# Probabilities, values and sums of squares as pairs of float32r halves in a three-block transformer kernel

## The chip, the core and the metric

The kernel runs on one core of a Trainium2 chip. The core has a matrix engine (TensorE, in the profile PE, with its weight loads as PEld), a vector engine (VectorE, DVE), a scalar engine (ScalarE, ACT), a general engine (GpSimd, POOL) and a queue that starts transfers (SyncE, SP). Each engine runs its own instructions in the order in which they were written; a semaphore makes one wait for another. Products are made in eight banks of PSUM, all else lies in SBUF. The metric is the device time of one execution in microseconds, as the median of several runs.

## The reference, cut to what matters

512 tokens of 1024 features pass through two layers of a first block and one layer of a second. The parts that the change touches are these:

```python
def rmsnorm(x, g, eps=EPS):
    y = xf * lax.rsqrt(jnp.mean(xf * xf, axis=-1, keepdims=True) + eps)
    return y * g
def memory_attention(q, mem_n, w_mem_kv, q_gain, k_gain):      # both layers, 4 heads of 64, 256 memory tokens
    kv = einsum('bmd,de->bme', mem_n, w_mem_kv)
    qh, k = rmsnorm(q, q_gain), rmsnorm(k, k_gain)
    p = softmax(einsum('bshd,bmhd->bhsm', qh, k) * 64 ** -0.5)
    o = einsum('bhsm,bmhd->bshd', p, v)
def diff_attention(q1, q2, k1, k2, v, lam):                    # second layer, 6 heads, values of 128 features
    p = softmax(mask(s1)) - lam * softmax(mask(s2))            # per tile of 128 queries, keys up to the diagonal
    o = einsum('bhqk,bkhe->bqhe', p, v)
# then o = rmsnorm(o, subln) per head; x = x + [o, memory o] @ w_o; x = x + squared-relu mlp(rmsnorm(x))
```

The second block (a convolution, a stick-breaking attention and a gated mlp) is computed by the same kernel; the change does not touch its arithmetic.

## The kernel before

Values lie feature-major, [128 features, 512 tokens]. Nearly every product of a weight matrix is made from float32r halves: a value x is held as a high half (x rounded to float32r, written by ScalarE in `high`) and a low half (x minus the high half, written by VectorE in `low`), and `mm3` adds three products, high by high, high by low and low by high. The weights come from memory in chunks of 128 x 1024 (tile `wr`), and `cut` makes their halves (`wh`) the same way, with three such tiles in flight. A chunk with the products on it is a unit; units run in a fixed order.

Some products are left in plain float32, one instruction in the program and two in the trace each. Among these are, in the first block: the sums of squares of the residual's norm (`norm_end`, tile `ms`, 512 columns, five times), of the keys' norm (`k_norm`, tile `hms` from the selecting constant `sel`, two per pair of key tiles), of the heads' output norm at the end of `diff_item` (tile `dms`), and probabilities by values in `mem_item` (tile `mpv`, values `mv`) and `diff_item` (tile `dpv`, values `v`). Probabilities come out of a transpose on PE (tile `ptr`) and are copied by ACT into `pT` for two tiles of tokens.

Stage B, the mixer of the second layer, is the place that the prediction is about. Its units are, in this order (`B_ORDER`): keys and queries of two pairs of heads (tile `k`, two times 48 + 48 products of 512 columns), the values of four heads (tile `v`, 96 + 96 products of 256 columns), the memory queries (48), keys and queries of the third pair (48 + 48), the last values (96), and then two parts of the output projection w_o (tile `g`): the part of heads 0 to 3 and of the memory attention (144 products), and the part of heads 4 and 5 (48). The first part of w_o needs the outputs of heads 0 to 3 and of the memory attention: its unit calls `need` on their flags before its first product is written into the program.

The order of the work beside the units is made by a planner when the program is built. Attention is written as generators (`diff_item`: one head, one tile of 128 queries, 24 of them; `mem_item`: two heads, one tile of tokens, 8 of them; `k_norm`, `q_norm`, `rope` and others), each of which yields a condition with `when`: tiles that it needs, and how many PSUM banks (`b=`) or tiles of SBUF (`u=`) must be free. After each slice of a unit's products `step` lets those go on whose condition holds at the planner's own estimate of time. Items wait in a queue, at most five are in flight (`INB`), and a new one needs nine free tiles (`ROOM`) of the 67 (`NSLOT`). Where a unit calls `need`, `until` writes the remaining steps of the generators one after another until the flags are set, with no product of a unit between them.

Of the kernel before, what the change touches and what calls it, by code (L numbers as in the profile page):

```python
# [9 lines left out]
F32 = mybir.dt.float32  # L10
F32R = mybir.dt.float32r
# [18 lines left out]
# columns of the packed per-partition vectors  # L30
# [12 lines left out]
# constants that follow from the shapes: for all phases, and for the two attention mixers  # L43
# [43 lines left out]
# the rotation's partners within 32 rows, where a pair of heads has its rotated features: 48 to 64 of one, 64 to 80 of the other  # L87
# [5 lines left out]
# the order of the chunks in the two attention mixers  # L93
# [21 lines left out]
class Token:  # L115
    """Counts a tile of a pool as in use for as long as something holds it."""
# [9 lines left out]
class View:  # L126
    """A tile or a part of one."""
# [22 lines left out]
class Engine:  # L150
    """An engine that also estimates when its instructions end (ns): the order of the work follows from that."""
# [4 lines left out]
    def cost(self, name, out, ins):  # L156
# [5 lines left out]
        # operands with one value per partition besides the tensors  # L162
# [32 lines left out]
class Chunk:  # L195
    """A half of a chunk of weights in tiles of 512 columns."""
# [9 lines left out]
class Unit:  # L206
    """A chunk of weights and the tensor engine's work on it, in slices."""
# [5 lines left out]
class K:  # L213
    def __init__(self, ctx, tc, a, out, stage=99):
# [12 lines left out]
        # emission: units, generators beside them with what each waits for, and queued ones  # L227
# [26 lines left out]
    def pair(self, n=T, s="s"):  # L254
        """A value's high and low halves in float32r."""
# [24 lines left out]
    def drop(self, *banks):  # L280
        """After the last instruction that uses these banks."""
# [35 lines left out]
    def spawn(self, g):  # L317
        """Work that goes on beside the chunks: a generator, a part of it whenever what it waits for is there."""
# [48 lines left out]
    def until(self, test, soft=False):  # L367
        """Goes on with the work beside the chunks until test() holds; soft: or nothing can go on."""
# [20 lines left out]
    def written(self, *tiles):  # L389
        """The tiles' values are under way: instructions that read them may follow."""  # L390
# [57 lines left out]
    def split_later(self, to, src, scale=None, f=None):  # L448
        """The halves, each when what it is made from is there."""
# [16 lines left out]
    def came(self, t, n):  # L466
        """A tile with n words per partition that a load brings."""
# [3 lines left out]
    def cut(self, c):  # L471
        """A chunk of weights as high and low halves; a gain goes by blocks of columns."""
# [30 lines left out]
    def mm3(self, ps, w, x, first, last, **kw):  # L503
        """ps += w.T @ x, each given as (high, low)."""
# [36 lines left out]
    def gemm_k(self, aps, n, xs, m, evac, gain=None, need=(), room=0):  # L541
        """Units that go over the contraction, [128 features, 512] in m banks."""
# [23 lines left out]
    def gemm_v(self, aps, xs, V, keys, gain=None, need=()):  # L566
        """Units for 256 features of the values with tokens on partitions, in two banks; V[key of 128 features, tile]."""
        st = {"d": 0}
        for c, ap in enumerate(aps):
            def body(w, c=c):  # L570
# [15 lines left out]
                if c == len(aps) - 1:  # L586
                    self.need(*need)
                    vs = [self.tmp(s="v") for j in range(2)]
                    for j in range(4):
                        v = vs[j // 2][:, j % 2 * M:(j % 2 + 1) * M]  # L590
                        self.act.activation(v, ps[j], AF.Copy, scale=self.tr[:, j:j + 1])
                        for n, key in enumerate(keys):
                            V[key, j] = v[:, n * P:(n + 1) * P]
# [1407 lines left out]
```

## Time and profile before

| | |
|---|---|
| time, median of 3 runs (lowest, highest) | 1780.07 us (1778.24, 1781.4) |
| span of the profiled execution | 1778.9 us |
| PE busy | 1756.0 us, 99% of the span, 8550 instructions |
| PEld busy | 1453.2 us, 82% |
| DVE busy | 1035.9 us, 58%, 1729 instructions |
| ACT busy | 764.4 us, 43% |
| HBM | 97 GB/s over the span |

The span runs from the first to the last instruction of the profiled execution; the median of the runs lies 1.2 us above it. Busy time is what an engine spent on instructions, with overlaps counted once; the ends of products are modelled, so that the distance from one start to the next tells more than a product's own duration. All arithmetic instructions are written through one helper and carry its line, L177, so the tiles' names tell them apart. "TILE<-A,B" is the tile that is written and what it is read from.

### The profile page before, as it was taken

Reading aid. Unit: us, or ns where it says so; the run is one execution under the profiler, and the core shown is the slowest. Engines: PE = TensorE matmul, PEld = TensorE weight load, DVE = VectorE, ACT = ScalarE, POOL = GpSimd, SP = SyncE. Lnnn points to the kernel's source line nnn. Section 1 sums busy time; section 2 is a strip of 40 time slices with the busy share of each in tenths; the row PEclk is TensorE's granted clock in tenths of the full one; section 3 lists DMA queues with packets and bytes.
Section 4 is the critical chain, followed back from the end, with each engine's and each line's share of the span. In section 5 each row is a group of like instructions: output and inputs, shape, how many; then the busy total and the mean of one; then the engine's idle time right before and its main releaser. Section 6 shows DMA issues by size and latency. Waiting matters only on the chain.

```text
span 1778.9 us, 21781 instructions
## 1 busy us (share of the span) xinstructions
PE 1756.0 (99%) x8550; PEld 1453.2 (82%) x8550; DVE 1035.9 (58%) x1729; ACT 764.4 (43%) x1371; POOL 0.2 (0%) x4
## 2 busy tenths in 40 slices
PE   8999999999999999999999999999999999999997
PEld 7888888888887887887888888887878988888887
DVE  7765654444455777857453535578984753244446
ACT  7543422222234678654222223457676632232234
POOL 0000000000000000000000000000000000000000
PEclk9999999999999999999999999999989999999998
DMA  5423222233233311152323222431112332232232
GB/s 202 141 70 96 95 95 95 97 99 101 95 116 127 104 48 45 57 195 96 95 95 100 101 96 95 142 98 48 60 48 83 99 127 96 95 103 97 95 108 94
DMA packets 57415, 175.71 MB, mean 99 GB/s; under 512 B 6752, under 2 KB 10080, under 8 KB 57312
## 3 DMA queue, kind: packets, MB, share of 16 engines
q1 hardware_dynamic: 57312, 174.32, 29.7%
q8 instruction: 67, 1.10, 0.2%
q14 instruction: 36, 0.29, 0.1%
HBM read 162.50 MB, written 10.22 MB: 97 GB/s over the span
## 4 chain that ended last, share of the span: by engine, by line
PE 96%; ACT 2%; DVE 1%; DMA 0%; SPq 0%; issue 0%; DVEq 0%; ACTq 0%
PE g L177 74%; PE k L177 8%; PE v L177 3%; PE z L177 2%; PE dsc L177 2%; PE mkv L177 1%; PE spv L177 1%; PE ptr L177 1%; PE mpv L177 1%; PE hms L177 1%; PE dpv L177 1%; PE ms L177 1%; ACT ez L177 0%; PE msc L177 0%; PE dms L177 0%; DMA x<-xd 0%
## 5 line engine op out<-in xcount | busy, mean ns | idle before, releaser
L177 PE MATMUL g<-xnh,wh 128*128 128x512 f32 x2176 | 687.9, 393 | 0.0
L177 ACT ACTIVATE wh<-wr 128x1024 fp32r<-128x1024 f32 (+2 forms) x259 | 271.5, 1048 | 650.5 <-PE g L177 490.2
L177 PEld LDWEIGHTS g<-xnh,wh 128*128 128x128 f32 x2176 | 410.4, 189 | 86.0 <-issue 0.7
L177 PE MATMUL g<-xnl,wh 128*128 128x512 f32 x1088 | 425.2, 391 | 1.7 <-DVE xnl L177 1.7
L177 PE MATMUL g<-ush,wh 128*128 128x512 f32 (+1 forms) x1304 | 400.3, 387 | 0.0
L177 DVE TENSOR_TENSOR wh<-wr,wh 128x1024 fp32r<-128x1024 f32 (+2 forms) x259 | 312.9, 1208 | 122.2 <-ACT wh L177 122.2
L177 PEld LDWEIGHTS g<-ush,wh 128*128 128x128 f32 x1304 | 244.2, 188 | 49.8
L177 PE MATMUL g<-usl,wh 128*128 128x512 f32 (+1 forms) x652 | 252.4, 387 | 0.0
L177 PEld LDWEIGHTS g<-xnl,wh 128*128 128x128 f32 x1088 | 205.4, 189 | 45.3 <-DVE xnl L177 2.5
L177 DVE TENSOR_TENSOR x<-x,g 128x512 f32<-128x512 f32 x88 | 60.2, 686 | 204.1 <-PE g L177 204.1
L177 DVE SCALAR_TENSOR_TENSOR u<-g,nr 128x512 f32<-128x512 f32 x84 | 58.0, 691 | 170.0 <-PE g L177 169.8
L177 PEld LDWEIGHTS g<-usl,wh 128*128 128x128 f32 x652 | 122.4, 188 | 25.0
L177 PE MATMUL k<-xnh,wh 128*128 128x512 f32 (+1 forms) x352 | 113.1, 390 | 5.7 <-ACT wh L177 5.7
L177 PEld LDWEIGHTS k<-xnh,wh 128*128 128x128 f32 x352 | 65.8, 192 | 20.5 <-ACT wh L177 5.7
L177 DVE SCALAR_TENSOR_TENSOR y<-glu,vec,y 128x510 f32<-128x510 f32 (+28 forms) x116 | 79.4, 728 | 0.9 <-ACT y L177 0.9
L177 ACT ACTIVATE ush<-u 128x512 fp32r<-128x512 f32 (+1 forms) x88 | 54.6, 623 | 36.3 <-DVE u L177 36.3
L177 PE MATMUL g<-Eh,wh 128*128 128x512 f32 (+1 forms) x208 | 67.2, 387 | 0.0
L177 PE MATMUL k<-xnl,wh 128*128 128x512 f32 (+1 forms) x176 | 66.3, 377 | 0.0
L177 PE MATMUL v<-wh,xnh 128*128 128x256 f32 x320 | 61.3, 291 | 0.0
L177 DVE TENSOR_TENSOR usl<-u,ush 128x512 fp32r<-128x512 f32 (+1 forms) x88 | 58.7, 671 | 0.0
L177 PEld LDWEIGHTS v<-wh,xnh 128*128 128x128 f32 x320 | 49.7, 191 | 1.3 <-issue 0.8
L177 ACT ACTIVATE g<-g 128x512 f32<-128x512 f32 (+1 forms) x24 | 14.3, 596 | 78.6 <-DVE g L177 78.6
(282 smaller groups left out, 2036.0 us busy)
## 6 DMA issues: line engine op xcount, KB each, us to landing
wr<-in_w_up SPq DMA_DIRECT2D x84, 512.0 KB, 3.4
wr<-in_w_down SPq DMA_DIRECT2D x80, 512.0 KB, 3.4
wr<-in_w_gate SPq DMA_DIRECT2D x20, 512.0 KB, 3.4
wr<-in_a_w_in SPq DMA_DIRECT2D x16, 512.0 KB, 3.9
wr<-in_w_in SPq DMA_DIRECT2D x16, 512.0 KB, 3.5
xd<-x SPq DMA_DIRECT2D x31, 256.0 KB, 2.0
x<-xd SPq DMA_DIRECT2D x31, 256.0 KB, 4.8
wr<-in_w_o SPq DMA_DIRECT2D x10, 512.0 KB, 3.5
```

The source lines that it names most:

```text
L177: r = f(out, *args, **kw)
```

## The change

Probabilities and values in both attentions of the first block become pairs of float32r halves, and their products become `mm3`, three float32r products for one float32 product. The values' low halves (`vl`, `mvl`) and the probabilities' low halves (the second half of `pT`) are new VectorE instructions that read PSUM. The sums of squares of full width (`ms`, `hms` of the keys, `dms`) are first split by a new generator `halves` (tile `hl`, one ACT and one DVE instruction of 512 columns and a `when` between them) and are then made by `mm2`, two float32r products against a constant in float32r. In `k_norm` the two key tiles are split one after the other. A pair of 512 columns takes two of the 67 tiles where a float32 value took one, so the values of stage B take twelve tiles in place of six, each layer's memory values two in place of one. `pT` grows from 4 to 8 KB per partition; the scratch for dynamic DMA is set to 1024.

```diff
     def probs(self, st, g):
...
-            st["pT", g] = View(self.pp.tile([P, 4, M], F32, tag="pt", name=self.name("pT")), Token(self.live, "pt"))
+            st["pT", g] = View(self.pp.tile([P, 2, 4, M], F32R, tag="pt", name=self.name("pT")), Token(self.live, "pt"))
...
+    def mm2(self, ps, w, x, first=True, last=True):
+        self.pe.matmul(ps, w, x[0], start=first, stop=False)
+        self.pe.matmul(ps, w, x[1], start=False, stop=last)
+    def halves(self, src, s="hl"):
+        o = self.pair(s=s)
+        self.high(o, src)
+        yield self.when(o[0])
+        self.low(o, src)
+        return o
...
     def gemm_v(...)
-                    vs = [self.tmp(s="v") for j in range(2)]
-                    for j in range(4):
-                        v = vs[j // 2][:, j % 2 * M:(j % 2 + 1) * M]
-                        self.act.activation(v, ps[j], AF.Copy, scale=self.tr[:, j:j + 1])
...
+                    vs = [self.pair(s="v") if halves else (self.tmp(s="v"),) for j in range(2)]
+                    for half in (self.high, self.low)[:1 + halves]:
+                        for j in range(4):
+                            v = [x[:, j % 2 * M:(j % 2 + 1) * M] for x in vs[j // 2]]
+                            half(v, ps[j], self.tr[:, j:j + 1])
...
     def norm_end(self, f, heads=False, tokens=False):
...
-        yield self.when(lambda: [st["last"]] if "last" in st else None, b=RESERVE + 1 + tokens)
+        yield self.when(lambda: [st["last"]] if "last" in st else None)
         acc = st["last"]
+        hl = yield from self.halves(acc)
+        yield self.when(*hl, b=RESERVE + 1 + tokens)
         ms = self.bank(s="ms")
-        mm(ms, self.onesd, acc, start=True, stop=True)
+        self.mm2(ms, self.onesdr, hl)
...
     def k_norm(self, st, out, f):
-        yield self.when(st["sk0"], st["sk1"], b=RESERVE + 1)
+        hl = []
+        for u in range(2):
+            yield self.when(lambda: [st[f"sk{u}"]] if f"sk{u}" in st else None)
+            hl.append((yield from self.halves(st[f"sk{u}"])))
+            del st[f"sk{u}"]
+        yield self.when(*hl[0], *hl[1], b=RESERVE + 1)
...
-            self.pe.matmul(m4[:4], self.c("sel")[:, 4 * u:4 * u + 4], st.pop(f"sk{u}"), start=u == 0, stop=u == 1)
+            self.mm2(m4[:4], self.selr[:, 4 * u:4 * u + 4], hl[u], u == 0, u == 1)
...
     def mem_item(...)        # diff_item alike
-        self.act.activation(pT[:, :, i % 2 * P:(i % 2 + 1) * P], pt.rearrange("p (j q) -> p j q", j=4), AF.Copy)
+        qs = slice(i % 2 * P, (i % 2 + 1) * P)
+        src = pt.rearrange("p (j q) -> p j q", j=4)
+        to = pT[:, 0, :, qs], pT[:, 1, :, qs]
+        self.high(to, src)
+        yield self.when(pT)
+        self.low(to, src)
...
-                self.pe.matmul(po[b], vv[:, m * M + t * P:m * M + (t + 1) * P], pT[:, 2 * b + m], start=m == 0, stop=m == 1)
+                vc = slice(m * M + t * P, m * M + (t + 1) * P)
+                self.mm3(po[b], (vv[0][:, vc], vv[1][:, vc]), (pT[:, 0, 2 * b + m], pT[:, 1, 2 * b + m]), m == 0, m == 1)
...
     def diff_item(...)
-            self.pe.matmul(po[:, c], V[h, j], pT[:, j, c], start=j == 0, stop=j == k - 1)
+            self.mm3(po[:, c], V[h, j], (pT[:, 0, j, c], pT[:, 1, j, c]), j == 0, j == k - 1)
...
-        yield self.when(sq, b=RESERVE + 1)
+        yield self.when(sq)
+        hl = yield from self.halves(sq)
+        del sq
+        yield self.when(*hl, b=RESERVE + 1)
         p2 = self.bank(s="dms")
-        self.pe.matmul(p2, self.onesh, sq, start=True, stop=True)
+        self.mm2(p2, self.oneshr, hl)
...
-    nc = bacc.Bacc("TRN2", target_bir_lowering=False, num_devices=1)
+    nc = bacc.Bacc("TRN2", target_bir_lowering=False, num_devices=1, dynamic_dma_scratch_size=1024)
```

Since the planner sets the order, the new steps and the scarcer tiles also move instructions. PE in stage B, at the 228th product of the units of stage B (in the values of heads 0 and 1, tile `v`): before, the first scores of the differential attention (`dsc`, keys `kh`/`kl` by queries `qh`/`ql`) stand here.

```order
L177 MATMUL v_4596<-wh_4480,xnh_3901 128x256 x2
L177 MATMUL v_4596<-wh_4480,xnl_3902 128x256
L177 MATMUL dsc_4649<-kh_4529,qh_4499 128x128
L177 MATMUL dsc_4649<-kl_4530,qh_4499 128x128
L177 MATMUL dsc_4649<-kh_4529,ql_4500 128x128
L177 LDWEIGHTS rmask
L177 MATMUL dsc_4649<-cmask,rmask 128x64
```

In the change the same place on PE holds a key norm (`hms` from the halves `hl`) and the spreading of the other one (`hb`).

```order
L177 MATMUL v_4646<-wh_4548,xnh_3963 128x256 x2
L177 MATMUL v_4646<-wh_4548,xnl_3964 128x256
L177 MATMUL hms_4698<-hlh_4570,selr 4x512
L177 MATMUL hms_4698<-hll_4571,selr 4x512
L177 MATMUL hms_4698<-hlh_4619,selr 4x512
L177 MATMUL hms_4698<-hll_4620,selr 4x512
L177 MATMUL hms_4703<-cst,hsq_4642 128x2 x4
L177 MATMUL hb_4708<-rhh_4622,selT 128x512
L177 MATMUL hb_4708<-rhl_4623,selT 128x512
```

The first `dsc` has moved behind 132 more products of `v`, to the 360th product of the stage.

PE where the output projection w_o begins (tile `g` from the heads' outputs `Eh`/`El`), before: between the last product of `v` and this place stand 59 rows, with the tail of the memory attention and the scores of heads 4 and 5.

```order
L177 MATMUL dsc_6332<-kh_6164,qh_6143 128x128
L177 MATMUL dsc_6332<-kl_6165,qh_6143 128x128
L177 MATMUL dsc_6332<-kh_6164,ql_6144 128x128
L177 LDWEIGHTS rmask
L177 MATMUL dsc_6332<-cmask,rmask 128x64
L177 MATMUL g_6343<-Eh_5191,wh_5936 128x512
```

PE at the same place in the change (`mpv` and `dpv` are the products of the probabilities `pT` by the values' halves).

```order
L177 MATMUL mpv_6572<-pT_6473,mvh_639 128x256 x2
L177 MATMUL mpv_6572<-pT_6473,mvl_640 128x256
L177 MATMUL mpv_6572<-pT_6473,mvh_639 128x256 x2
L177 MATMUL mpv_6572<-pT_6473,mvl_640 128x256
L177 MATMUL ptr_6592<-cst,e_6556 128x128 x3
L177 MATMUL dpv_6607<-pT_6542,vh_6005 128x256 x2
L177 MATMUL dpv_6607<-pT_6542,vl_6006 128x256
L177 MATMUL dpv_6607<-pT_6542,vh_6005 128x128 x2
L177 MATMUL dpv_6607<-pT_6542,vl_6006 128x128
L177 MATMUL g_6616<-Eh_5619,wh_5737 128x512
```

Here 180 rows stand between the last product of `v` and the first of w_o: the end of heads 2 and 3 and all eight memory items have moved into this stretch, without a product of a unit among them.

## Rows read from the trace of the kernel before

**Rows 1.** The page, part 1: busy us, share and instructions of each engine.

```profile
PE 1756.0 (99%) x8550; PEld 1453.2 (82%) x8550; DVE 1035.9 (58%) x1729; ACT 764.4 (43%) x1371; POOL 0.2 (0%) x4
```

**Rows 2.** Busy time by stretch: stretch, us, busy us per engine, granted clock, DMA share, GB/s.

```profile
610.00:720.00 110.00, 109.73 (x668) 88.31 (x668) 88.64 (x238) 82.65 (x222) 0.00 (x0) 1.00 0.18 55
720.00:807.00 87.00, 86.03 (x450) 69.69 (x448) 60.28 (x131) 48.73 (x108) 0.00 (x0) 1.00 0.39 129
```

**Rows 3.** The chain that ended last: start us, us, what (instructions of the trace).

```profile
94.25 1.73 PE mpv L177 x8
...
212.07 341.38 PE g L177 x1506
...
763.15 1.52 PE dpv L177 x8
...
768.87 0.86 PE dms L177 x2
...
1187.90 7.19 PE v L177 x60
```

**Rows 4.** Instructions of PE in order of time: start us, us, instruction.

```profile
611.53 0.27 PE L177 MATMUL dsc<-kl,qh 64*128 64x128 f32 x1
611.64 0.27 PE L177 MATMUL dsc<-kh,ql 64*128 64x128 f32 x1
```

**Rows 5.** Groups of VectorE, 553 to 807 us: shapes, count, busy us, mean ns, idle.

```profile
L177 DVE TENSOR_REDUCE nm<-dsc 128x1 f32<-128x512 f32 x12 | 8.0, 687 | 1.3 <-PE dsc L177 0.7
L177 DVE TENSOR_SCALAR e<-e,rs 128x256 f32<-128x256 f32 x22 | 7.1, 351 | 0.5
L177 DVE TENSOR_REDUCE nm<-msc 128x1 f32<-128x256 f32 x16 | 6.0, 415 | 3.3 <-PE msc L177 3.3
L177 DVE RECIPROCAL rs<-ssum 128x2 f32<-128x2 f32 x32 | 5.1, 159 | 8.7 <-ACT e L177 8.4
L177 DVE TENSOR_TENSOR kl<-vg,kh 128x512 fp32r<-128x512 f32 x6 | 4.0, 683 | 0.7 <-ACT kh L177 0.7
L177 DVE TENSOR_TENSOR mol<-mpv,moh 64x256 fp32r<-64x256 f32 x8 | 3.4, 420 | 0.3 <-ACT moh L177 0.2
```

**Rows 6.** The chain again, stage B: first scores, and the stretch ahead of w_o.

```profile
611.44 3.18 PE dsc L177 x24
...
721.38 0.56 PE msc L177 x6
...
732.79 0.44 PE ptr L177 x4
733.22 3.46 PE mpv L177 x16
...
737.12 3.19 PE dsc L177 x24
...
742.23 1.76 PE dsc L177 x8
...
745.18 1.59 PE g L177 x6
```

**Rows 7.** Busy time in two stretches in which VectorE is busiest, columns as in Rows 2.

```profile
710.00:720.00 10.00, 10.00 (x75) 8.69 (x74) 9.72 (x24) 8.61 (x24) 0.00 (x0) 1.00 0.30 91
1320.00:1330.00 10.00, 8.69 (x38) 6.60 (x37) 10.00 (x19) 9.19 (x23) 0.00 (x0) 0.83 0.01 2
```

**Rows 8.** Busy time behind a run of scores of 64 rows, columns as in Rows 2.

```profile
1232.00:1236.00 4.00, 4.00 (x16) 2.80 (x16) 4.00 (x7) 3.81 (x10) 0.00 (x0) 0.72 0.00 0
1304.00:1308.00 4.00, 4.00 (x10) 3.08 (x10) 2.42 (x5) 3.03 (x9) 0.00 (x0) 0.50 0.00 0
```

**Rows 9.** The first norm: two instructions in order of time, and the chain.

```profile
27.43 0.69 ACT L177 ACTIVATE ra<-ms,eps 128x512 f32<-128x512 f32 x1 [0.86 <-PE ms L177]
...
30.82 0.68 DVE L177 TENSOR_SCALAR eb<-ms 128x512 f32<-128x512 f32 x1
...
32.43 2.72 PE mkv L177 x12
```

More of the change, by code (lines that the diff above doesn't have):

```diff
@@ L564, in gemm_k, with gemm_v @@
             self.add(ap, body, None if gain is None else gain[:, c * k:(c + 1) * k])
-    def gemm_v(self, aps, xs, V, keys, gain=None, need=()):
+    def gemm_v(self, aps, xs, V, keys, gain=None, need=(), halves=False):
         st = {"d": 0}
@@ L587, in body @@
                     self.need(*need)
-                    vs = [self.tmp(s="v") for j in range(2)]
-                    for j in range(4):
-                        v = vs[j // 2][:, j % 2 * M:(j % 2 + 1) * M]
-                        self.act.activation(v, ps[j], AF.Copy, scale=self.tr[:, j:j + 1])
-                        for n, key in enumerate(keys):
-                            V[key, j] = v[:, n * P:(n + 1) * P]
+                    vs = [self.pair(s="v") if halves else (self.tmp(s="v"),) for j in range(2)]
[3 more added lines that the diff above has]
+                            half(v, ps[j], self.tr[:, j:j + 1])
+                            for n, key in enumerate(keys):
+                                o = [x[:, n * P:(n + 1) * P] for x in v]
+                                V[key, j] = o if halves else o[0]
                     self.drop(*st.pop("ps"))
@@ L636, in norm_end @@
         st = self.sum
-        yield self.when(lambda: [st["last"]] if "last" in st else None, b=RESERVE + 1 + tokens)
+        yield self.when(lambda: [st["last"]] if "last" in st else None)
         acc = st["last"]
+        hl = yield from self.halves(acc)
+        yield self.when(*hl, b=RESERVE + 1 + tokens)
         ms = self.bank(s="ms")
-        mm(ms, self.onesd, acc, start=True, stop=True)
+        self.mm2(ms, self.onesdr, hl)
+        del hl
         if tokens:
@@ L710, in run @@
         self.onesd, self.onesh, self.onesc = fill("onesd", 1.0 / D), fill("onesh", 1.0 / P), fill("onesc", 1.0 / T)
+        self.onesdr, self.oneshr = self.const(cp, "onesdr", F32R, self.onesd), self.const(cp, "oneshr", F32R, self.onesh)
         self.nr = cp.tile([P, T], F32, name="nr")
@@ L802, in evac @@
                 self.pe.matmul(pr[:, i:i + 1], st["acc"][:, i * P:(i + 1) * P], self.onesd[:, 0:1], start=True, stop=True)
-            self.mem = [([self.pair(M, "kT") for _ in range(2)], self.tmp(s="mv")) for _ in range(2)]
+            self.mem = [([self.pair(M, "kT") for _ in range(2)], self.pair(s="mv")) for _ in range(2)]
             def rest():
@@ L812, in rest @@
                     for i in range(2):
-                        self.spawn(self.mem_keys(l, i, ps[2 * l + i], mr, self.mem[l][0], self.mem[l][1][:, i * M:(i + 1) * M]))
+                        self.spawn(self.mem_keys(l, i, ps[2 * l + i], mr, self.mem[l][0], [x[:, i * M:(i + 1) * M] for x in self.mem[l][1]]))
             st.clear()
@@ L838, in mem_keys @@
         self.act.activation(sq, ps[:, :M], AF.Square, scale=mr[:, i:i + 1])
-        self.act.activation(v, ps[:, M:], AF.Copy, scale=mr[:, 2 + i:3 + i])
+        self.high(v, ps[:, M:], mr[:, 2 + i:3 + i])
         ss = self.small(4, "kss")
@@ L842, in mem_keys @@
         self.dve.tensor_reduce(ss, sq.rearrange("p (h d) -> p h d", h=4), axis=AX.X, op=ALU.add)
+        self.low(v, ps[:, M:], mr[:, 2 + i:3 + i])
         yield self.when(ss)
@@ L917, in k_norm @@
     def k_norm(self, st, out, f):
-        yield self.when(st["sk0"], st["sk1"], b=RESERVE + 1)
+        hl = []
[4 more added lines that the diff above has]
+        yield self.when(*hl[0], *hl[1], b=RESERVE + 1)
         m4 = self.bank(s="hms")
         for u in range(2):
-            self.pe.matmul(m4[:4], self.c("sel")[:, 4 * u:4 * u + 4], st.pop(f"sk{u}"), start=u == 0, stop=u == 1)
+            self.mm2(m4[:4], self.selr[:, 4 * u:4 * u + 4], hl[u], u == 0, u == 1)
+        hl = None
         yield self.when(m4, self.eb)
@@ L957, in mem_item @@
         tk = slice(i * P, (i + 1) * P)
-        yield self.when(q[0], q[1], r, *kT[t], vv, b=RESERVE + 2, u=ROOM)
+        yield self.when(q[0], q[1], r, *kT[t], *vv, b=RESERVE + 2, u=ROOM)
         ps = [self.bank(M, "msc") for _ in range(2)]
@@ L1093, in inputs @@
             yield self.when(self.cst)
+            self.selr = self.const(self.cp, "selr", F32R, self.c("sel"))
             self.selT = self.const(self.cp, "selT", F32R, self.c("selT")[:4])
@@ L1301, in plan_b @@
                 w = a[f"w_v{seq[1]}"]
-                self.gemm_v([w[c] for c in range(2)], xs, V, (2 * seq[1], 2 * seq[1] + 1), gkv, need=("nBt",))
+                self.gemm_v([w[c] for c in range(2)], xs, V, (2 * seq[1], 2 * seq[1] + 1), gkv, need=("nBt",), halves=True)
             elif seq[0] == "qm":
@@ L1366, in diff_item @@
         pT = self.probs(st, g)
-        self.act.activation(pT[:, :i + 1, i % 2 * P:(i % 2 + 1) * P], pt.rearrange("p (j q) -> p j q", j=i + 1), AF.Copy)
+        qs = slice(i % 2 * P, (i % 2 + 1) * P)
+        src = pt.rearrange("p (j q) -> p j q", j=i + 1)
+        to = pT[:, 0, :i + 1, qs], pT[:, 1, :i + 1, qs]
+        self.high(to, src)
+        yield self.when(pT)
+        self.low(to, src)
         self.drop(pt)
@@ L1373, in diff_item @@
         k = 2 * g + 2
-        yield self.when(pT, lambda: [V[h, j] for j in range(k)] if (h, 3) in V else None, b=RESERVE + 1)
+        yield self.when(pT, lambda: [x for j in range(k) for x in V[h, j]] if (h, 3) in V else None, b=RESERVE + 1)
         po = self.bank(M, "dpv")
@@ L1395, in diff_item @@
         st.clear()
-        yield self.when(sq, b=RESERVE + 1)
+        yield self.when(sq)
+        hl = yield from self.halves(sq)
+        del sq
+        yield self.when(*hl, b=RESERVE + 1)
         p2 = self.bank(s="dms")
-        self.pe.matmul(p2, self.onesh, sq, start=True, stop=True)
+        self.mm2(p2, self.oneshr, hl)
+        del hl
         yield self.when(p2)
```

## The prediction

> **What bounds the kernel now.** I read the page's busy shares first. PE is busy for 1756.0 of 1778.9 us [rows 1], so on the whole every microsecond taken from PE's products is a gain, and work put on VectorE (58%) or ScalarE (43%) is free. But shares are means over stages, so I read busy time by stretch next. In stage B VectorE is at 88.64 of 110 us while PE is full [rows 2], and in single stretches of 10 us at 97 to 100% [rows 7]. The reader is to see that the change adds most of its VectorE work where least of it is left over. Third I read the chain that ended last for the price of each kind of product, and last how the order moved on PE, which decides this case.
>
> **What the products save.** Prices come from the chain, where a piece's length over its count is the pace [rows 3]. A float32r product of 512 columns takes 341.38/1506 = 0.227 us, one of 256 columns 7.19/60 = 0.120. A plain float32 product of 512 columns takes 0.86 (`dms`). Of these there are 17 (five `ms`, six `hms` of the keys, six `dms`), each replaced by two float32r products: 17 x (0.86 - 0.45) = 7.0 us saved. Probabilities by values: a memory group (four float32 products, eight trace instructions) takes 1.73 us now and 12 x 0.120 = 1.44 then; eight groups save 2.3. A wide head group (three products of 256 columns, one of 128) takes 1.52. Narrow float32r products of 128 columns follow each other after 0.11 us [rows 4], so 9 x 0.120 + 3 x 0.11 = 1.41; six groups save 0.7. A narrow head group (256 and 128 columns) takes 3/7 of 1.52 = 0.65 by its columns and then 0.69: six groups lose 0.2. Together 9.8 us are saved if PE never waits for what is new.
>
> Rows 4 show that a float32r product of 128 columns is hardly cheaper than one of 256. [...]
>
> **What is added elsewhere.** By the built order the change adds 76 VectorE instructions: 17 low halves of sums of squares at 0.683 us (the like of `kl` [rows 5]) = 11.6; 40 of the probabilities, 15,872 columns at 0.683 per 512 = 21.2; 16 of the values at 0.42 (`mol`, which also reads PSUM) = 6.7; three casts. That is 39.5 us, nothing against 1779, and most of it lies in stage B. No row shows a low half of 512 columns read from PSUM; its ends are 0.683 (`kl`, from SBUF) and twice 0.42 = 0.84 (`mol`). I take 0.683, since `kl` has all 128 partitions and the same width. ScalarE gets 17 instructions more.
>
> **The first norm.** Its chain of two halves lies behind PE's last products of the first unit, so `ms` stands 12 products (2.7 us) later, and the memory products start 12 products sooner after it. From `ms` at work on ScalarE (27.43) to the release of its bank (31.5) pass 4.1 us, and the third bank of `mkv`, wanted 1.4 us after 32.43, had 2.3 us in hand [rows 9]. 2.7 and about 0.5 us for later semaphores exceed that by 0.9 us: I book a wait of 0.9 (0 to 2). The other four norms have products of free banks behind them.
>
> **Stage B.** Here the price of the change is not in its instructions but in where attention stands. Each `when` costs the planner at least one slice of products, `k_norm` now has four more of them, and values held as pairs leave fewer free tiles for a new item. The order shows the result: the first scores stand 132 value products later, and the products of w_o, which need heads 0 to 3 and the memory attention, stand behind 180 rows without a unit's product where there were 59. I follow the time through it.
>
> (a) First scores: 611.44 before [rows 6]. 132 x 0.120 = 15.8 later; saved until there 4.0 (three `ms` 1.2, four `hms` 1.6, four memory groups 1.2); lost 0.9 at the first norm and 0.4 for one query norm moved ahead. So 624.5.
>
> (b) To the last value product: before, 611.44 to 733.2, 121.8 us without a wait. Now 15.8 less for the value products already done, 3.9 saved (four `dms` 1.6, memory 1.2, wide heads 0.3, the third pair's `hms` 0.8), 0.9 added by steps moved ahead, and 18.3 moved behind the last value product (30.3 against 12.0, below). That leaves 84.7, to 709.2. VectorE's rows there come to about 75 us, 88% as before, so no wait is booked.
>
> (c) The stretch ahead of w_o. PE, before: 733.22 to 745.18, 12.0 us [rows 6], all of it work. PE now: 84 products of probabilities by values x 0.120 = 10.1; 48 memory scores, 0.56 for six, 4.5; 47 transposes x 0.11 = 5.2; seven items' scores, 3.19 + 1.76 for four of them, 8.7; eight sums and spreadings at 0.23, 1.8: 30.3 us. VectorE must write 127 instructions between the scores that open this stretch and the last `mol`: 24 wide ones at 0.683, 16.4; 11 score maxima, 4,608 columns at 0.687 per 512, 6.2; 16 memory maxima at 6.0/16, 6.0; 17 multiplications at 7.1/22, 5.5; eight `mol` at 0.42, 3.4; 35 small ones at 0.159, 5.6; 16 others, 5,888 columns at 0.683, 7.9: 51.0 us [rows 5]. So PE no longer sets the pace here. With VectorE at 98% (the mean of 97 and 100% of rows 7) the stretch takes 52 us, PE waits for 22 of them, and w_o begins at 761.2 in place of 745.18: 16.0 us late.
>
> (d) Afterwards the rest is saved: two `dms` 0.8, two `ms` 0.8, and 1.3 of attention that now lies ahead of w_o: 2.9. The tail's `dms` stands 54 products, 12 us, ahead of the part of w_o that needs it, so its longer chain is covered. Against that 1.0 for TensorE's clock: scores of 64 rows alone let the granted clock fall to half, and it stayed there for the products that followed (0.72 and 0.50 [rows 8]).
>
> The sum, on the profiled execution: 1778.9 + 16.0 - 2.9 + 1.0 = 1793.0. The median of the runs lies 1.2 above the span, so **1794 us**. Its own range: VectorE's rows may overlap at their seams (48 us in place of 52) or VectorE may be held up by ScalarE and PE and reach only 85% (60 us); 0.84 for the wide low halves adds 2. With 2 us for (a) that is 1787 to 1805.
>
> **The rivals.** *The plain sum (faster).* VectorE keeps up, PE never waits in the stretch ahead of w_o, and 9.8 - 0.9 = 8.9 us are saved: 1771. For it speaks that before PE waited there not at all; it decides if those 127 instructions take no longer than PE's 30.3 us, 0.24 us each where the rows give 0.40. *Half of the cover.* The stretch takes about 40 us, because work that I place in it is already done while PE makes the last values; then w_o begins 4 us late and the sum gives 1782. Against it: the scores that feed that work stand in the stretch itself. *Half clock through the whole stretch.* PE's 30.3 us are mostly scores of 64 rows, transposes and waits; at half pace they would be 60.6, PE would again be the bound, and w_o would begin 10 us later than booked: 1803 to 1812. For it speak rows 8. [...] *The new products run in two passes each, as the old ones.* Then 108 + 34 products cost as much again; rows 3 show float32r products of 256 columns at 0.120, so I give it no chance of its own.
>
> **How the numbers follow.** The forecast 0.62, half clock 0.18, half of the cover 0.10, the plain sum 0.10. A measurement of this kernel tells 0.2% from no change, 1776.5 to 1783.6. So faster 0.10, same 0.10, slower 0.80. The range holds the forecast's own, the half cover and the half clock up to 1810: 1779 to 1810.
>
> **What would show it.** Right: in the changed kernel PE waits some 20 us for VectorE (or ScalarE) between the last `v` and the first w_o product, VectorE is above 90% there, first scores come near 624 and w_o near 761, and `mpv` groups take 1.4 us, `dms` 0.45. Wrong: first scores at 624 but w_o before 750 means that VectorE's work was overpriced or done earlier; a wait spread over 625 to 709 means that it was already the bound in (b); a loss behind the second layer means a cause that I have not seen.

## The result, and the profile after

The changed kernel takes 1791.03 us in the median (1790.81 to 1794.82), the kernel before 1780.19 beside it: a ratio of 1.0069, 95% interval 1.0057 to 1.0082. It is slower, 3 us under the forecast of 1794 and inside the range. The profiled execution spans 1793.0 us, the figure of the sum. That agreement is luck: this execution is the longest of the four (the others span 1789.0 to 1789.4 us), two errors of about 1.6 us cancel in it, and one of the sum's reasons fell; the last two are below.

The page's first part of the changed kernel, busy us, share and instructions of each engine:

```profile
PE 1759.7 (98%) x8618; PEld 1466.9 (82%) x8618; DVE 1070.8 (60%) x1805; ACT 773.3 (43%) x1388; POOL 0.2 (0%) x4
```

PE is busy for 3.7 us more than in [rows 1], although its products became cheaper. Busy time counts products at half clock too (the trace has a granted clock of 1.00 or 0.50, and by their mean over the span 0.985 here and 0.994 before), so here it isn't work. Busy time by stretch of the same kernel, columns as in [rows 2]:

```profile
610.00:720.00 110.00, 107.39 (x660) 92.06 (x658) 88.16 (x229) 75.37 (x195) 0.00 (x0) 0.94 0.20 61
720.00:807.00 87.00, 79.80 (x421) 64.13 (x422) 71.98 (x173) 54.51 (x135) 0.00 (x0) 0.90 0.23 76
626.00:712.50 86.50, 85.77 (x496) 72.30 (x495) 67.25 (x179) 58.89 (x156) 0.00 (x0) 0.92 0.19 60
712.50:762.80 50.30, 41.22 (x246) 32.56 (x245) 48.54 (x133) 37.99 (x105) 0.00 (x0) 0.86 0.05 14
```

Up to 720 VectorE has about what it had (88.16 for 88.64 us). Behind 720 it has 71.98 in place of 60.28, and in the stretch between the last value product and w_o (last row) it is busy for 48.54 of 50.3 us, 96%, while PE has holes and a granted clock of 0.86. The chain of work that ended last of the changed kernel: start us, us, what.

```profile
626.27 3.18 PE dsc L177 x24
629.46 2.64 PE v L177 x12
...
633.25 2.87 PE v L177 x12
...
688.28 1.36 PE dpv L177 x12
...
701.43 4.51 PE v L177 x24
...
738.51 1.19 DVE pT L177 x2
739.70 0.67 DVE nm L177 x2
740.38 0.02 issue
740.40 0.16 DVE nm L177
740.56 0.09 DVE rs L177
740.64 0.02 issue
740.67 0.62 DVE e L177 x2
741.28 0.61 DVE rb L177
...
745.99 2.90 PE mpv L177 x12
...
762.82 2.58 PE g L177 x6
```

Where [rows 6] had PE pieces alone, the chain now runs from 712.5 to 745.9 through VectorE pieces, with two gaps of 0.9 us together: low halves (`pT`), score maxima (`nm`), reciprocals and divisions (`rs`, `e`), the heads' norm (`rb`). This is what a VectorE that sets the pace looks like. From 746 to 756 the chain is PE's again, in part at half clock (from 745.7 to 749.1 it is 0.50, and 12 `mpv` products take 2.90 us; at 1.00 they take 1.63 from 752.6 and 1.43 from 110.0). The first scores stand at 626.3, w_o begins at 762.8.

### The profile page after: what moved, and what is told of

It reads as the page before. It is cut to its first block, busy times and chain, and to the rows that moved or that the text cites. A ratio compares the mean times of both kernels' runs of the same rounds, so it can differ in the third digit from the quotient of the medians.

```text
span 1793.0 us, 22017 instructions
## 1 busy us (share of the span) xinstructions
PE 1759.7 (98%) x8618; PEld 1466.9 (82%) x8618; DVE 1070.8 (60%) x1805; ACT 773.3 (43%) x1388; POOL 0.2 (0%) x4
## 4 chain that ended last, share of the span: by engine, by line
PE 93%; DVE 4%; ACT 2%; DMA 0%; issue 0%; SPq 0%; DVEq 0%; ACTq 0%
PE g L177 73%; PE k L177 8%; PE v L177 3%; PE z L177 2%; PE dsc L177 1%; PE mkv L177 1%; PE spv L177 1%; DVE nm L177 1%; PE hms L177 1%; PE mpv L177 1%; PE ptr L177 1%; PE dpv L177 1%; DVE e L177 0%; ACT ez L177 0%; PE ms L177 0%
## 5 line engine op out<-in xcount | busy, mean ns | idle before, releaser
L177 PEld LDWEIGHTS g<-usl,wh 128*128 128x128 f32 x652 | 122.4, 188 | 24.8
L177 DVE SCALAR_TENSOR_TENSOR y<-glu,vec,y 128x510 f32<-128x510 f32 (+28 forms) x116 | 79.4, 727 | 0.9 <-ACT y L177 0.9
L177 PEld LDWEIGHTS v<-wh,xnh 128*128 128x128 f32 x320 | 54.0, 206 | 1.9 <-issue 1.4
```

The costliest lines, as they stand in the source:

```text
L177: r = f(out, *args, **kw)
```

## The experiments

Stage B begins in every kernel with the same `k` product, at 551.3 to 554.5 us by the chains (553.45 before, 554.14 changed). The table counts w_o's first product from there, so that earlier stages don't enter. First scores, w_o and VectorE's busy time come from one profiled execution of each kernel, which may lie off the median: by 3.8 us above it for the changed kernel, 3.1 for e10 and 5.6 for e12, by 4.8 below it for e2, 2.7 for e3 and 3.6 for e9. Between two rows of these columns a few us can therefore be chance. "Ahead" is the number of PE instructions between the last product of a unit and w_o; the last column is VectorE's busy time from the first scores to w_o over that stretch's length.

| kernel | median us | ratio to before (95%) | first scores | w_o from start of B | ahead | VectorE |
|---|---|---|---|---|---|---|
| before | 1780.2 | 1 | 611.4 | 191.7 | 61 | 105.9/133.7 |
| changed | 1791.0 | 1.0069 (1.0057 to 1.0082) | 626.2 | 208.6 | 243 | 115.7/136.5 |
| e1 keys undone | 1787.2 | 1.0041 (1.0028 to 1.0054) | 611.5 | 202.6 | 159 | 123.0/145.1 |
| e2 keys alone | 1779.4 | 0.9994 (0.9984 to 1.0004) | 622.0 | 193.0 | 122 | 99.5/123.4 |
| e3 values alone | 1788.1 | 1.0043 (1.0030 to 1.0055) | 609.5 | 203.4 | 156 | 124.9/145.5 |
| e4 norms alone | 1779.9 | 0.9998 (0.9986 to 1.0009) | 612.0 | 190.1 | 59 | 106.7/132.6 |
| e5 no low halves | 1779.4 | 0.9995 (0.9986 to 1.0004) | 626.0 | 195.6 | 243 | 104.3/123.5 |
| e6 scaling on ScalarE | 1807.9 | 1.0142 (1.0121 to 1.0163) | 626.2 | 224.2 | 243 | 103.4/152.1 |
| e7 covered parts | 1776.5 | 0.9983 (0.9973 to 0.9993) | 609.2 | 190.5 | 59 | 106.7/132.6 |
| e8 keys, one wait | 1790.0 | 1.0050 (1.0037 to 1.0063) | 609.2 | 208.2 | 194 | 129.6/152.7 |
| e9 low halves added | 1789.5 | 1.0064 (1.0048 to 1.0081) | 611.2 | 200.6 | 61 | 117.9/142.7 |
| e10 covered parts, keys | 1780.2 | 1.0006 (0.9997 to 1.0016) | 607.2 | 198.6 | 101 | 112.6/142.8 |
| e11 VectorE load | 1780.7 | 1.0000 (0.9989 to 1.0010) | 610.4 | 193.6 | 61 | 116.0/135.7 |
| e12 load twice | 1785.1 | 1.0036 (1.0024 to 1.0049) | 611.5 | 198.6 | 61 | 129.2/140.7 |

The expectations name these theories. A, the prediction's: VectorE sets the pace ahead of w_o, both because the scores come late and because of the low halves. B: the late scores alone. C: VectorE's load by the low halves alone. D: the halved products or the norms' longer chains. E: the order on PE, with its handing over between engines. F: the low halves hold VectorE up until ScalarE has written the high half. All kernels of the experiments, those built on the kernel before too, have the wider `pT` and the scratch of 1024, so these two are not the cause: e11, which has nothing else of the change but VectorE instructions added, takes no longer than the kernel before.

**Which part of the change costs?** Four kernels undo parts of it.

e1 takes the keys' halves out of the changed kernel:

```
-            hl.append((yield from self.halves(st[f"sk{u}"])))
+        yield self.when(st["sk0"], st["sk1"], b=RESERVE + 1)
-            self.mm2(m4[:4], self.selr[:, 4 * u:4 * u + 4], hl[u], u == 0, u == 1)
+            self.pe.matmul(m4[:4], self.c("sel")[:, 4 * u:4 * u + 4], st.pop(f"sk{u}"), ...)
```

> The changed kernel with the sums of squares of the keys back in plain float32 products (six hms, no halves, no added waits in k_norm). By the order the first scores stand again at the 228th product of stage B, and 159 PE instructions lie ahead of w_o (changed kernel 243, kernel before 61). Theory A (VectorE sets the pace of what is piled up ahead of w_o, from both causes, late scores and low halves; PE idles about 20 us for 182 more instructions, 0.11 us for each): 98 x 0.11 = 10.8 idle, 7.3 saved by products, 1 at the first norm: 1785. Theory B (the late start of the scores alone makes the loss): 1774. Theory C (the low halves of probabilities and values alone load VectorE): 1790, w_o near 762.

e2 is the kernel before with that part alone added (the same lines, signs exchanged):

> The kernel before with the keys' sums of squares in halves and nothing else of the change (six low halves, 4.1 us of VectorE). First scores 108 products of v later, 122 PE instructions ahead of w_o. Theory A: 61 x 0.11 = 6.7 idle, 2.5 saved: 1784. Theory B: scores 13 us late, nearly all of it seen at w_o: 1788 to 1790. Theory C: 4.1 us more on VectorE are covered, 2.5 saved: 1778.

e3 takes all sums of squares out of the changed kernel (the lines of e1, and those of e4 below with signs exchanged):

> The changed kernel with all sums of squares back in plain float32; probabilities and values of both attentions stay in halves. First scores where they stood before, 156 PE instructions ahead of w_o. Theory A: 95 x 0.11 = 10.4 idle, 2.8 saved: 1788. Theory B: 1777. Theory C: 1790.

e4 keeps only the halves of the norms and of the heads:

```
-        mm(ms, self.onesd, acc, start=True, stop=True)
+        self.mm2(ms, self.onesdr, hl)
...
-        self.pe.matmul(p2, self.onesh, sq, start=True, stop=True)
+        self.mm2(p2, self.oneshr, hl)
```

> The kernel before with only the five sums of squares of the norms (ms) and the six of the heads (dms) in halves. Scores and the 59 PE instructions ahead of w_o stand as before. All theories that lay the loss to stage B: 11 x 0.41 = 4.5 saved, 1 to 2 lost at the first norm: 1777, with w_o near 744. Theory D (the products of halves themselves cost more than the rows say, or their longer chains make PE wait at each norm): 1780 to 1784.

Measured: 1787.2, 1779.4, 1788.1 and 1779.9. The keys alone move the first scores to 622 and cost nothing that can be measured, so theory B falls. The values alone bring 8 of the 11 us with the scores where they stood. Theory A was near for e1 and e3, but predicted 1784 for e2, where 122 instructions ahead of w_o give 1.3 us: a price per instruction isn't the right measure. Theory C held best, except that the keys add 4 us to the values (1791.0 against 1787.2). e4 gives no sign that the halved sums cost more than booked in themselves: w_o is 1.6 us earlier. Of the 4.5 us that it was to save, some 2 went at the first norm (below), and where the rest went no run shows.

**Does it matter where the scores stand?** e8 is the changed kernel with one wait of the planner in `k_norm` in place of four; the instructions are the same.

```
+        yield self.when(st["sk0"], st["sk1"])
+        hl = [self.pair(s="hl") for u in range(2)]
         for u in range(2):
-            yield self.when(lambda: [st[f"sk{u}"]] if f"sk{u}" in st else None)
-            hl.append((yield from self.halves(st[f"sk{u}"])))
+            self.high(hl[u], st[f"sk{u}"])
+        for u in range(2):
+            self.low(hl[u], st.pop(f"sk{u}"))
```

> The changed kernel with the keys' four halves written behind one wait of the planner instead of four: the first scores are back at the 228th product, 194 instructions ahead of w_o in place of 243; the same instructions on every engine. Theory A (late scores add to the loss): 3.9 us of idle time more than with the keys undone (35 x 0.11) and 2.5 saved: 1788.6. Theory C (VectorE's load alone; where the scores stand doesn't matter): 1791.

The scores begin at 609.2 again, 17 us before those of the changed kernel, and w_o comes at 208.2 against 208.6: 1790.0. The stretch ahead of w_o is shorter (41.1 us for 50.3), and what was saved there is lost ahead of it. Busy time of e8 from the first scores to the last value product, and from there to w_o:

```profile
609.00:720.80 111.80, 109.41 (x695) 93.59 (x695) 90.99 (x243) 76.59 (x205) 0.00 (x0) 0.95 0.19 60
720.80:761.90 41.10, 33.58 (x195) 26.26 (x195) 38.77 (x105) 30.36 (x84) 0.00 (x0) 0.83 0.07 26
```

VectorE is at 81 and 94%, PE at a clock of 0.83 in the second row. Where attention begins is therefore not the cause; theory A had 1788.6 here, C 1791.

**Are the low halves the cause?** e5 has every instruction of PE and ScalarE in the changed kernel's order and leaves out the 40 low halves of the probabilities; the third product of a group reads the high half again, so the low half doesn't enter the values.

```
         yield self.when(pT)
-        self.low(to, src)
...
-   ... (pT[:, 0, j, c], pT[:, 1, j, c]), j == 0, j == k - 1)
+   ... (pT[:, 0, j, c], pT[:, 0, j, c]), j == 0, j == k - 1)
```

> The changed kernel with every instruction of PE and ScalarE in its place, but without the 40 low halves of the probabilities on VectorE (14 of them, 8.1 us, in the stretch ahead of w_o). Left out of the computation: the third product of each group reads the high half again, so the low half of the probabilities doesn't enter the values. Theory A/C (VectorE's instructions set the pace of that stretch): it shortens from 50.3 us to about 42, and the time from 1791 to 1783, or to 1780 where the 7 us taken ahead of the stretch shorten it too. Theory E (not VectorE's load but the order on PE: each item passes PE, VectorE, ScalarE, VectorE and PE in turn, and PE waits through these steps): 1789 to 1791.

1779.4: 11.7 us come back, as the second figure of theory A/C (1780) had it, and theory E (the order alone) falls as the cause of the loss. But nothing is saved either: the rival of the plain sum had 1771 for the same products, and these 8 us are lost without any low half of the probabilities. w_o begins 13.0 us sooner, and the low halves that the changed kernel wrote between first scores and w_o are 13.7 us (8.1 behind the last value product, 5.6 ahead of it). Busy time of e5 in the two stretches:

```profile
626.00:705.40 79.40, 79.40 (x496) 66.82 (x495) 62.75 (x167) 58.85 (x156) 0.00 (x0) 1.00 0.21 65
705.40:749.50 44.10, 39.40 (x244) 31.07 (x242) 41.59 (x118) 36.97 (x101) 0.00 (x0) 0.85 0.06 16
```

Half of the gain lies ahead of the last value product (79.4 us for 86.5): there PE now runs without a hole and at full clock, where the changed kernel had 0.92.

e6 takes as much from VectorE in another way, the divisions by the sums, and gives it to ScalarE:

```
-            self.dve.tensor_scalar(e[:, sl], e[:, sl], rs[:, b:b + 1], None, op0=ALU.mult)
+            self.act.activation(e[:, sl], e[:, sl], AF.Copy, scale=rs[:, b:b + 1])
```

> The changed kernel with every instruction of PE in its place; the division of the probabilities by their sums (e by rs, 22 instructions and 7.4 us of VectorE in the stretch ahead of w_o) is done by ScalarE instead. Theory A/C: VectorE needs 40.7 us there, ScalarE with 38 + 9 us becomes nearly as busy; the time falls to 1784. Theory E: one more change of engine in each item, 1790 to 1793.

1807.9, 17 us slower than the changed kernel instead of 7 faster, and far beyond theory E too. VectorE's waits of e6 from the first scores to w_o, and ScalarE's: engine, line, waited for: us in total, times, longest.

```profile
DVE e L177 <- ACT e L1391: 25.7, 19, 5.5
```

```profile
ACT e L1391 <- DVE rs L177: 12.2, 9, 3.2
ACT e L1005 <- DVE rs L177: 5.6, 5, 1.5
```

Each item now goes from VectorE (`rs`) to ScalarE (`e`) and back, and the engines wait for each other by turns: VectorE stands for 25.7 us behind ScalarE, ScalarE for 17.8 behind VectorE. VectorE has only 103.4 us of work in 152.1. A lighter VectorE is of no use if it must wait; so it isn't the sum of its busy time alone that counts.

**Load, or place in the chain?** Two kernels put the same VectorE instructions into the kernel before, and a third puts in twice as many, with every instruction of PE and ScalarE as there. In e9 the low half is written behind the copy of the probabilities, and nobody reads it:

```
         self.act.activation(pT[:, :, qs], src, AF.Copy)
+        self.nc.vector.tensor_sub(lo[:, :, qs].ap, src.ap, pT[:, :, qs].ap)
```

> The kernel before with every instruction of PE and ScalarE in its place, in plain float32, and 40 VectorE instructions more: the low half of each piece of the probabilities is written beside it and read by nobody (21.2 us by 0.683 us for 512 columns; 32 of them, 15.7 us, in stage B). Theory C (VectorE's load sets when w_o can begin, whatever PE's products cost and wherever the scores stand): VectorE has 105.9 of 133.7 us between first scores and w_o; the changed kernel and its relatives got no further than 85% there, so 120 us need 141: w_o 8 us late, or up to 11, 1788 to 1791. Rival (the halved products, or the order that the planner gives them, make the loss; VectorE has 27.8 us free there): 1780 to 1782.

1789.5, as theory C had it. VectorE's waits of e9 from the first scores to w_o, its chain ahead of w_o, and busy time around the hole in PE:

```profile
DVE pT L1390 <- ACT pT L177: 13.4, 8, 4.0
DVE pT L1007 <- ACT pT L177: 3.5, 1, 3.5
```

```profile
739.74 0.69 DVE pT L1007
740.43 0.86 DVE wh L177
741.29 0.09 DVE rs L177
...
742.53 5.10 PE dsc L177 x24
747.63 3.37 PE mpv L177 x8
```

```profile
735.00:742.00 7.00, 4.40 (x25) 3.67 (x24) 3.39 (x10) 6.04 (x18) 0.00 (x0) 1.00 0.00 0
742.00:748.00 6.00, 6.00 (x29) 4.86 (x30) 5.46 (x16) 2.46 (x8) 0.00 (x0) 0.64 0.34 112
```

VectorE stood for 16.9 us before these writes until ScalarE had written the high half, with its next work queued behind. In all it is idle no longer there than in the kernel before (24.8 us and 27.8); what has changed is what stands behind the wait. So e9 alone doesn't tell load from place. e11 issues the same number of instructions of the same widths when the products are issued, on tiles long written:

```
         yield self.when(pT, b=RESERVE + 2)
+        for z in range(2):
+            qs, nj = slice(z * P, (z + 1) * P), 4
+            self.nc.vector.tensor_sub(lo[:, :nj, qs].ap, pT[:, :nj, qs].ap, pT[:, :nj, qs].ap)
```

> The kernel before with every instruction of PE and ScalarE in its place and the same 40 VectorE instructions more as in the kernel with the low halves added (21.2 us by 0.683, some 13 of it between the start of stage B and w_o), but issued when the products of the probabilities are, on tiles long written, so that VectorE waits for nothing on their account. Theory C, by the runs so far: w_o begins 45 us after as much VectorE work as lies between the start of stage B and w_o (163.2 and 208.6 us in the changed kernel, 157.6 and 203.4 with the values alone, 151.8 and 195.6 without the low halves), or after 191 us of PE's own work where that is more. 138.9 + 13 = 152, so 197, 5 us late: 1785. Rival F (the low halves cost by holding up VectorE until ScalarE has written the high half, not by their length): 1780 to 1781.

e12 issues them twice (a loop of two around these lines):

> As the kernel with the plain VectorE load, with 80 such instructions (42.4 us, some 27 of it between the start of stage B and w_o). Theory C: 138.9 + 27 = 166, so 211, 19 us late: 1799. Rival F: the 27.8 us that VectorE has free between first scores and w_o take most of it, 1780 to 1785.

1780.7 and 1785.1: the plain load costs nothing measurable once (ratio 1.0000), and 6.4 us by the ratio twice, at the upper end of what rival F had. Busy time from first scores to w_o, of e11 and of e12:

```profile
610.40:746.10 135.70, 135.23 (x827) 109.64 (x826) 115.98 (x311) 98.29 (x265) 0.00 (x0) 0.99 0.18 57
```

```profile
611.50:752.20 140.70, 138.76 (x827) 111.75 (x826) 129.18 (x342) 98.62 (x265) 0.00 (x0) 0.96 0.18 55
```

e11 and e9 have nearly the same VectorE time (116.0 and 117.9 us) and the same PE order, and differ by 8.8 us in time. Theory C in the form "w_o comes 45 us after VectorE's work" falls (197 and 211 predicted, 193.6 and 198.6 measured); rival F holds for e11. It is e12 that decides this, since the VectorE time that the traces show from the start of stage B to w_o, 148.9 and 162.1 us, makes that form 194 and 207. In the kernel before, VectorE takes 13 us of instructions more (10 by busy time) as long as nobody waits for it there.

**What is worth keeping?** e7 has the halves in the four later norms, in the heads and in the memory attention of the first layer; the first norm, the keys and stage B's probabilities and values are plain float32.

```
+        if tokens:
+            mm(ms, self.onesd, acc, start=True, stop=True)
+        else:
+            self.mm2(ms, self.onesdr, hl)
...
+                if l == 0:
+                    self.mm3(po[b], (vv[0][:, vc], vv[1][:, vc]), (pT[:, 0, 2 * b + m], pT[:, 1, 2 * b + m]), m == 0, m == 1)
+                else:
+                    self.pe.matmul(po[b], vv[0][:, vc], pT[:, 2 * b + m], start=m == 0, stop=m == 1)
```

> The parts of the change that lie in stretches with VectorE to spare and behind no short wait: halves in the sums of squares of the four later norms and of the heads, and in the memory attention of the first layer (ten sums, four groups); the first norm, the keys and all of stage B's values stay plain float32. Order around w_o as in the kernel before (59 instructions ahead of it). All theories: 10 x 0.41 + 1.2 = 5.3 saved and nothing lost, 1775 (1774 to 1777). If the first norm cost nothing, 1779 as the kernel with all eleven sums in halves (1779.9) less 0.8.

e10 adds the keys' halves behind one wait to e7 (the lines of e8):

> The parts without a price (four later norms, heads, memory attention of the first layer) and the keys' halves behind one wait, the rest plain float32; 101 instructions ahead of w_o in place of 59. Six more sums in halves save 2.5 on PE and put 4.1 us of VectorE into stage B. Theory C: VectorE is then near 85% between first scores and w_o, and the 2.5 come back as waits: 1776 to 1777, as without the keys. If stage B has room left: 1774.

e7 takes 1776.5, 0.9983 of the kernel before (0.9973 to 0.9993): faster than both kernels, if only by 3 us and less than the 5.3 booked. e10 takes 1780.2: the keys, or the order that comes with them, take it all back, 3.7 us, although they save 2.5 on PE. Both expectations (1776 to 1777, and 1774) missed that. Busy time and chain of e10 ahead of w_o, in an execution 3.1 us above its median:

```profile
724.00:728.00 4.00, 1.01 (x5) 0.41 (x3) 3.90 (x13) 2.46 (x10) 0.00 (x0) 0.97 0.36 129
728.00:732.00 4.00, 2.95 (x12) 2.49 (x13) 3.87 (x12) 1.44 (x4) 0.00 (x0) 0.50 0.50 164
732.00:736.00 4.00, 4.00 (x16) 3.15 (x16) 2.47 (x7) 1.87 (x5) 0.00 (x0) 0.67 0.00 0
736.00:740.00 4.00, 3.75 (x26) 3.14 (x25) 1.39 (x6) 2.48 (x9) 0.00 (x0) 1.00 0.01 4
740.00:744.00 4.00, 4.00 (x19) 2.69 (x18) 3.57 (x11) 3.59 (x12) 0.00 (x0) 0.68 0.00 0
744.00:748.00 4.00, 4.00 (x12) 2.87 (x12) 3.76 (x12) 0.86 (x3) 0.00 (x0) 0.50 0.00 0
```

```profile
731.96 3.20 PE mpv L177 x8
...
738.27 3.18 PE dsc L177 x24
...
742.49 3.17 PE dsc L177 x8
745.66 3.22 PE mpv L177 x8
```

PE stands for 3 us while VectorE is full, and then works at a granted clock of 0.50 and 0.67: a group of `mpv` takes 3.20 in place of the 1.73 of [rows 3], 1.5 us on top of the wait. From 736 the granted clock is 1.00. It falls a second time, to 0.68 and 0.50, behind the 24 scores at 738.27, with hardly a hole (PE is busy for 7.75 of 8 us), and scores then take 3.17 in place of the 1.76 of [rows 6], a group 3.22.

## Why the prediction was right, and where it was wrong

**What the products save** was priced right piece by piece: a wide head group takes 1.36 (1.41 booked), a memory group 1.43 (1.44), where the clock is full. In the whole time only part of it could be shown: e7 saves 3.0 us (1.2 to 4.8) for 5.3 booked. Where the rest went no run settles. The same holds for the 8 us by which e5 stays behind the plain sum.

**The first norm** was mis-sized: 0.9 booked, 0 to 2. PE's waits of the changed kernel from 20 to 60 us, of which the kernel before has none:

```profile
PE mkv L177 <- DVE wh L177: 1.1, 1, 1.1
PE mkv L177 <- DVE eb L177: 0.5, 1, 0.5
PE mkv L177 <- DVE rb L177: 0.4, 1, 0.4
```

They make 2.0, the end of my range. The step counted the bank that `mkv` waits for, and not the cast of the next weights (`wh`, the wait of 1.1) that stands in VectorE's order behind the longer chain. Its 0.5 us for later semaphores were an estimate of mine that no row shows. e4 and e7, of which only e7 keeps the first norm plain, differ by as much: the first `g` products of the first layer begin at 58.0 and 56.1.

**Step (a)** gave 624.5 for the first scores, and they came at 626.3. Its reading fell: "the price of the change is not in its instructions but in where attention stands" is refuted for the scores by e2 (11 us later, nothing lost) and e8 (early again, as slow). The price is in the low halves.

**Step (b)** gave 709.2 for the end of the values, which was 712.5. Half of the 3.3 us came with (a). That the other half is so small is luck. In e5 the same 496 instructions of PE take 79.4 us without a hole at full clock, 5.3 less than the 84.7 booked. In the changed kernel they take 86.5: PE's holes are 0.7 us, the rest is clock, 0.92 in the mean. In its chain 12 `v` products take 2.64 and 2.87 us at a granted clock of 0.50 (629.7 to 636.5) and 24 of them 4.51 (0.50 to 704.8), where 12 take 1.43 at 1.00 in the kernel before (from 625.97). I had booked no wait and thought no further than waits.

**Step (c)** held in its sum. VectorE sets the pace ahead of w_o at 96% (98 booked), the stretch takes 50.3 us (52), w_o begins at 762.8 (761.2). What PE does meanwhile was wrong: not 22 us of waits, but 9 and a busy time of 41.2 for what I priced at 30.3. By the granted clock of 0.86 half clock makes an estimated 7 of these 11 us (it is 0.50 from 721.8 to 728.6, 732.1 to 735.5 and 745.7 to 749.1, in all 13.7 of 50.3 us, half of which is lost); the other 4 I had priced too low here, and (b) too high. The rival of half clock was thus at work, but under VectorE's cover: VectorE is idle for 1.8 us of the stretch, and by no more can half clock have lengthened it. One of the two rows behind the 98% lies at 1320 us, outside stage B; the 96% is the stage's own. e5 shows that the low halves make the loss, with PE's order held.

**What (c) left out** is that VectorE's load is no price by itself: off the chain it is harmless in the old order. By w_o's distance from the start of stage B: before 191.7; the load off the chain in the old order 193.6 (e11); the low halves behind their copies in the old order 200.6 (e9); the new order without low halves 195.6 (e5, in which by the booked prices some 5.5 us of saved products help); both 208.6. With e11 the single effects, 1.9 and 3.9, don't make 16.9; with e9 they are 8.9 and 3.9 and come to 12.8. So how much the order adds to the price of the low halves isn't settled; what follows is argued, not shown. In the old order an item's VectorE work is spread over 133 us of products of values, keys and queries, and VectorE has 27.8 us free there. In the new one 182 more PE instructions lie behind the last value product, and there is nothing else for PE to do while VectorE works off theirs. How much of the 11.7 us of e5 is VectorE's time, and how much that each item's products wait for the low half, stays open: in e9 the place in the chain cost 8.8 us more than the same time off it (e11), but e9 waits for ScalarE, and the low halves of the changed kernel hardly do. Their group ahead of w_o, columns as in [rows 5], has 0.1 us of idle time in front of it, at 0.686 us each (0.683 booked from SBUF):

```profile
L177 DVE TENSOR_TENSOR pT<-ptr,pT 128x512 fp32r<-128x512 f32 x9 | 6.1, 686 | 0.1
```

**Step (d)** gave 1.9 saved from w_o to the end; it was 3.5 (1030.2 us for 1033.7), which makes up, together with the shorter stretch of (c), for (b), so that the sum ended on 1793.0. The clock's 1.0 is there (the first `g` products take 2.58 for 1.59, at 0.50 from 762.8 to 766.2). Its reason was put too generally: behind the scores of 64 rows from 611.44 the kernel before keeps a granted clock of 1.00. The other 1.6 are within what this part differs from one execution to the next: e2, whose work behind w_o is the plain one of before, needed 1027.2. The sum is therefore less exact than it looks: against the spans of the other three executions it is 3.6 to 4.0 us too long. The median of the runs also lies 2.0 below the profiled span, where I had added 1.2. In the terms given, the forecast's own range is 1788 to 1806 and not 1787 to 1805, and the rival of two passes leaves out the memory's 96 products beside the 108 of the heads; neither decides anything here.

## What to carry to other kernels

Work added to an engine that is 79% busy beside a full PE could be free here (e11, a ratio of 1.0000) or cost most of its length (e9, a ratio of 1.0064, and the changed kernel against e5, 11.7 us). What told the two apart was whether it stands between two steps that somebody waits for (8.8 us between e9 and e11 at 117.9 and 116.0 us of VectorE) and, as it seems but is not shown, whether the order leaves PE other products meanwhile. Before a sum of saved products is believed, price the stretch in which the order has run out of independent work, there by the engine that feeds PE, and measure with PE's order held, once without the added instructions and once with them off the chain. Take the cheap parts of such a change (here the later norms, the heads and the first layer's memory attention) by themselves.

## What was not expected of the hardware

In e9 and e10 a short wait of PE is followed by products at a lower granted clock. In e9 PE is busy for 4.4 of 7 us, and in the next 6 the granted clock is 0.64: 24 score instructions take 5.10 us for 3.18, and a memory group 3.37 for 1.73, together 3.6 us behind a hole of 2.6. In e10 PE is busy for 1.01 of 4 us; in the next 8 us the granted clock is 0.50 and 0.67, and a group takes 3.20, 1.5 us more. The clock also fell without such a wait. In e10 it was back at 1.00 and went to 0.68 and 0.50 behind 24 scores, which cost 2.9 us. In the changed kernel the first scores are followed by `v` products at a granted clock of 0.50 (2.64 and 2.87 us for 12), while the same scores of the kernel before (3.18 us in both) are followed by 12 `v` products at 1.00 (1.63 us); what set the two apart is not settled.
